# A one-core transformer block with 32 streamed experts: weights packed in load order, the router on the residual's own sums, one modulation sum on ScalarE and GpSimd

## The chip, the cores and the metric

The kernel runs on one core of a Trainium2 chip (trn2). The metric is the device time of one launch in microseconds (us). The kernel before takes 1129.11 us, the median of 3 runs (1129.04 to 1129.2). The engines are named as the profile names them: PE (TensorE), PEld (its weight loads), DVE (VectorE), ACT (ScalarE), POOL (GpSimd) and SP (SyncE, which here only issues DMAs).

## What is computed

One block over 256 tokens of width 1024: a modulated mixer (attention with forget gates, gated linear attention, a multi-scale pool), a layer norm, a top-4 mixture of 32 experts, a second layer norm. All in float32. Cut to what matters:

```python
mod = silu(c) @ w_ada + b_ada                # 6 vectors of 1024
shift1, scale1, gate1, shift2, scale2, gate2 = split(mod, 6)
h = x * (1 + scale1) + shift1
y = hybrid_mixer(h, w_in, ..., w_out)        # z = h @ w_in; attention, GLA, pool; @ w_out
x = layer_norm(ALPHA * x + (1 + gate1) * y, ln1_g, ln1_b)
h = x * (1 + scale2) + shift2
y = moe_ffn(h, w_router, w_gate_up, w_down)  # top 4 of 32 experts by h @ w_router + b_router
x = layer_norm(ALPHA * x + (1 + gate2) * y, ln2_g, ln2_b)
```

The experts' weights (32 times a gate/up matrix of 1024x2048 and a down matrix of 1024x1024) are 402 of the 449 MB that the kernel moves.

## The kernel before, in words

All tokens sit on the core as 2 tiles of 128 (`TT = 2`, `t`), the width as 8 slices of 128 (`KT = 8`, `k`). A matmul goes through the helper `mm` (L134 in the profile, L156 after the change).

The stages, with their tiles:
- **First layer.** `load_ada1` brings the columns of `w_ada` for shift1 and scale1, `load_z1` rows of `w_in`; `tokens_to_columns` transposes x on PE (`xT`), `modulate` makes hT = h transposed, and a loop over k adds up `pqk` (q and k of the attention) and `pz`. `second_part(0)` and `second_part(1)` do the remaining columns of `w_in` (`pz20n`, `pz21n`, weights `wz2_0`, `wz2_1`).
- **Mixer.** Scores `sc0` (first 128 queries) and `sc1`, their row maxima `mx0`, `mx1`, exponentials on ACT with row sums (L490), normalisation on DVE (L491, L492), transposes `ppT0` to `ppT5` on PE, outputs `po`; the gated linear attention with states `st`/`sts`, masks `at0`, `at1` (L599) and outputs `pg0`, `pg1`.
- **Modulation sums.** shift2 and scale2 (`accm0`, `accm1`, weights `adam0`, `adam1`), gate1 (`acc1`, weights `adag1`) and gate2 (`g2p`, weights `adag2`) are each a sum over 8 slices, `acc += w_k * cond_k`: one multiplication, then 7 `scalar_tensor_tensor` (STT) on DVE (L546, L624). `pcol0` and `pcol1` are 8 small matmuls each that turn accm0 and accm1 into columns; `m2`, `hA`, `hB` (L550 to L553) are made from them.
- **Out projection and router.** `py` is the product with `w_out` (`wo0`, `wo1`), then the residual and the first norm to `n1`, transposes `ph`, modulated columns `h2T`, logits `plg`, top 4, positions of the tokens in each expert's slots (`posm`), counts.
- **Experts.** 16 pairs of experts. `dispatch` builds a 0/1 matrix `pp` and gathers a pair's tokens by matmul (`pxg`, then `xg`), `gate_up` makes `gu`, `down` makes `py`, `combine` adds into `ya`.

Every engine runs its instructions in one fixed order, which a scheduler sets when the program is built, from the written program and its dependencies; it is not the order of the source. An instruction that waits holds up everything behind it on its engine. SP's order is that of the loads in the source. A load into a ring buffer waits until the last reader of that buffer's earlier content is done. The ring has `NA = 5` buffers of 2 MB; from the experts on a second pool, `ring2`, adds `NB = 3` in the memory that the earlier stages leave.

The expert loads go on SP: four `g` (gate/up, `load_up`, L737) and two `d` (down, `load_down`, L742) of 2 MB for each expert, which wait only for buffers.

Of the kernel before, what the change touches and what calls it, by code (L numbers as in the profile page):

```python
# [104 lines left out]

def packed_rows(b_ada, ln1_g, ln1_b, ln2_g, ln2_b):
# [6 lines left out]
def block_kernel(ctx: ExitStack, tc, x, w_ada, w_in, gla_w_a2, pool_w, w_out, w_router, w_gate_up, b_gate_up,  # L113
# [48 lines left out]

    half = const.tile([P, 8], F32, name="half")
# [13 lines left out]


    with tc.tile_pool(name="early", bufs=1) as ea, tc.tile_pool(name="late", bufs=1, side="right") as la_, \
# [9 lines left out]
        def load_ada1(cc):  # L189
            t = ring_tile(f"ada1_{cc}")  # L190
            if cc == 0:
                t = t.rearrange("p (a k s n) -> p a k s n", a=2, k=KT, s=2)
                ada.append(t.rearrange("p a k s n -> p a k (s n)"))
                return [lambda a=a: [SY.dma_start(t[:, a, :, h], w_ada[0, :, h * D + a * P:h * D + (a + 1) * P]
                                                  .rearrange("(k p) n -> p k n", p=P)) for h in range(2)]
                        for a in range(2)]
# [4 lines left out]
            ada.append(t.rearrange("p k s n -> p k (s n)"))  # L201

        def load_z1(k):
            if k % 2 == 0:
                wz1.append(ring_tile(f"wz1_{k // 2}")[:, 0:2 * (C_FV + Z1)].rearrange("p (k n) -> p k n", k=2))
            t = wz1[-1][:, k % 2]
            SY.dma_start(t[:, 0:W1], w_in[0, k * P:(k + 1) * P, 0:W1])
            SY.dma_start(t[:, W1:], w_in[0, k * P:(k + 1) * P, C_GA:])

        def load_cols(j, nm):  # L210
            ts = []
            for i in range(2):
# [25 lines left out]
        bgf = []  # L238
        for h in range(2):
            bgf.append(la_.tile([96, 2, 512], F32, tag=("acc", "g1p")[h], name=f"bgf{h}"))  # L240
            for j in range(3):
                SY.dma_start(bgf[h][32 * j:32 * j + 32], b_gate_up[0, 16 * h:16 * h + 16]
# [21 lines left out]
        ada_m.append(load_cols(4, "adam1"))  # L264
        wo = {}
        for i, ks in enumerate(((0, 1, 2, 6), (7, 3, 4, 5))):
            t = ring_tile(f"wo{i}").rearrange("p (k n) -> p k n", n=D)
            for j, k in enumerate(ks):
                wo[k] = t[:, j]
            j, k = (0, 0) if i == 0 else (1, 3)  # L270
            SY.dma_start(t[:, j:j + 3], w_out[0, k * P:(k + 3) * P, :].rearrange("(k p) n -> p k n", p=P))
            j, k = (3, 6) if i == 0 else (0, 7)
            SY.dma_start(t[:, j], w_out[0, k * P:(k + 1) * P, :])
        SY.dma_start(wr.rearrange("p (i k) n -> p i k n", k=2), w_router[0].rearrange("(i p k) n -> p i k n", p=P, k=2))
# [15 lines left out]
        for h in range(2):  # L290
            three_terms(bg3[:, 2 * h:2 * h + 2], bgf[h])
# [8 lines left out]
        hT = la_.tile([P, KT, S], F32, tag="hT", name="hT")  # L300
# [48 lines left out]
        for k in range(KT):  # L349
# [19 lines left out]
        z2 = la_.tile([P, TT, ZN - O_GV], F32, name="z2")  # L369
# [10 lines left out]
        z_gv = z2[:, :, 0:GVW]  # L380
        z_gr = z2[:, :, GVW:]
# [689 lines left out]
```

## Time and profile before

| | us |
|---|---|
| median of 3 runs | 1129.11 (1129.04 to 1129.2) |
| the profiled execution, its own time | 1129.8 |
| its span on the core | 1128.0 |
| PE busy in the span | 1035.4 (92%) |
| DVE / ACT / POOL busy | 318.7 (28%) / 98.8 (9%) / 41.5 (4%) |
| mean granted PE clock | 0.982 of full speed |
| HBM read | 447.67 MB, mean 398 GB/s over the span |

Times in the rows are us from the start of the span. In a timeline row the first number is the start, the second how long the stretch lasted, then the engine, the line, the operation, the output and inputs by name, shapes and how many; in brackets the idle time before it and what ended it. Busy shares are averages over stages with different limits; what holds the kernel up must be read stage by stage.

### The profile page before, as it was taken

What the parts mean: (1) busy time and instruction counts of PE and PEld (TensorE: products, weight loads), DVE (VectorE), ACT (ScalarE), POOL (GpSimd) and SP (SyncE); (2) the same over time, 40 slices, a digit from 0 to 9 for tenths busy, and PEclk for the clock granted to TensorE, in tenths of its full rate; (3) what the DMA queues carried; (4) which work ended last, traced back from release to release, by engine and by line L of the source; (5) the groups of instructions that cost most, each with busy time, mean ns of one, the idle gap of its engine ahead of it and who ended that gap; (6) DMA issues with size and microseconds to landing.
All of it is one profiled execution on the core that took longest, in us unless ns stands there. A gap on an engine that the chain in (4) does not pass through costs nothing.

```text
span 1128.0 us, 11046 instructions
## 1 busy us (share of the span) xinstructions
PE 1035.4 (92%) x4734; PEld 436.9 (39%) x4735; DVE 318.7 (28%) x587; ACT 98.8 (9%) x205; POOL 41.5 (4%) x43
## 2 busy tenths in 40 slices
PE   6999998999999999996999999989989898989795
PEld 3656545434333333333344343423333333333231
DVE  1459694322222122211122221213221121211113
ACT  1024112100000000000000000000000000000100
POOL 2270000000000000000000000000000000000000
PEclk9999897999999999998999999999999999999998
DMA  9997499999999999999899999999999999999992
GB/s 324 348 385 283 181 378 373 428 423 428 428 428 427 428 428 428 428 427 423 344 427 428 428 428 426 428 427 428 428 428 427 428 429 427 428 427 428 428 414 92
DMA packets 52998, 449.49 MB, mean 398 GB/s; under 512 B 5056, under 2 KB 18768, under 8 KB 28496
## 3 DMA queue, kind: packets, MB, share of 16 engines
q1 hardware_dynamic: 52320, 447.90, 95.7%
q8 instruction: 39, 0.64, 0.2%
q10 hardware_dynamic: 624, 0.83, 0.2%
q14 instruction: 15, 0.12, 0.0%
HBM read 447.67 MB, written 1.05 MB: 398 GB/s over the span
## 4 chain that ended last, share of the span: by engine, by line
PE 29%; DMA 22%; DVE 1%; issue 1%; ACT 0%; POOL 0%; DVEq 0%; POOLq 0%
DMA d<-in_w_down 22%; PE gu L134 13%; PE py L134 7%; PE pxg L134 4%; PE ya L134 3%; PE pyl L134 1%; PE paT L837 1%; DVE yb L855 0%; DVE aT L839 0%; DVE res L919 0%; ACT n L931 0%; PE pln L134 0%; DVE r L1038 0%; DVE yl L1015 0%; DVE st L1019 0%
## 5 line engine op out<-in xcount | busy, mean ns | idle before, releaser
L134 PE MATMUL gu<-g,xg 128*64 128x512 f32 x2048 | 462.5, 595 | 14.0 <-DMA g<-in_w_gate_up 12.6
L134 PEld LDWEIGHTS gu<-g,xg 128*64 128x64 f32 x2048 | 143.2, 137 | 295.5 <-issue 261.0
L134 PE MATMUL py<-d,aT 128*64 128x512 f32 x992 | 227.1, 600 | 13.8 <-DMA d<-in_w_down 12.5
L825 DVE TENSOR_SCALAR g<-gu 128x512 f32<-128x512 f32 x32 | 22.1, 692 | 410.1 <-PE gu L134 410.1
L134 PEld LDWEIGHTS py<-d,aT 128*64 128x64 f32 x992 | 70.0, 137 | 150.5 <-issue 140.8
L134 PE MATMUL pxg<-pp,n 128*128 128x128 f32 x512 | 77.0, 302 | 14.9 <-DVE aT L839 7.0
L134 PEld LDWEIGHTS pxg<-pp,n 128*128 128x128 f32 x512 | 69.2, 208 | 43.0 <-issue 29.6
L855 DVE TENSOR_TENSOR yb<-py,g2p 64x512 f32<-64x512 f32 x60 | 41.3, 689 | 139.0 <-PE py L134 138.4
L134 PE MATMUL ya<-yb,sg_None 128*128 128x512 f32 x120 | 58.2, 607 | 4.9 <-DVE yb L855 4.8
L829 ACT ACTIVATE s<-g 128x512 f32<-128x512 f32 x32 | 20.2, 630 | 464.4 <-DVE g L825 464.4
L793 DVE TENSOR_SCALAR xg<-pxg,hA,hB 128x128 f32<-128x128 f32 x64 | 25.8, 409 | 99.2 <-PE pxg L134 90.0
L791 ACT ACTIVATE xg<-pxg,hB,hA 128x128 f32<-128x128 f32 x64 | 28.7, 457 | 274.3 <-DVE xg L793 273.6
L134 PE MATMUL pz<-wz,hT 128*128 128x512 f32 (+2 forms) x128 | 52.4, 547 | 0.0
L169 POOL TENSOR_TENSOR rsb<-rtb,half 128x2 f32<-128x2 f32 x1 | 0.7, 701 | 950.9 <-DVE rtb L168 950.9
L839 DVE COPY aT<-paT 128x512 f32<-128x512 f32 x32 | 22.1, 692 | 43.9 <-PE paT L837 43.8
L134 PE MATMUL py<-wo,oT 128*128 128x512 f32 x64 | 30.9, 629 | 0.2 <-ACT oT L642 0.2
L134 PEld LDWEIGHTS ya<-yb,sg_None 128*128 128x128 f32 x120 | 20.4, 189 | 26.9 <-issue 17.4
L134 PEld LDWEIGHTS pz<-wz,hT 128*128 128x128 f32 x128 | 23.4, 190 | 17.3 <-issue 14.3
L837 PEld LDWEIGHTS paT<-kc,l 128*128 128x128 f32 x128 | 18.0, 209 | 25.3 <-DVE l L831 15.4
L837 PE MATMUL paT<-kc,l 128*128 128x128 f32 x128 | 23.7, 308 | 0.0
L831 DVE TENSOR_TENSOR l<-l,s 128x512 f32<-128x512 f32 x32 | 22.1, 691 | 3.4 <-DVE l L830 0.5
L134 PE MATMUL pqk<-hT,wz 128*128 128x256 f32 x96 | 22.2, 381 | 0.7 <-DVE hT L332 0.7
(245 smaller groups left out, 519.1 us busy)
## 6 DMA issues: line engine op xcount, KB each, us to landing
g<-in_w_gate_up SPq DMA_DIRECT2D x128, 2048.0 KB, 30.4
d<-in_w_down SPq DMA_DIRECT2D x62, 2048.0 KB, 30.4
adam<-in_w_ada SPq DMA_DIRECT2D x4, 2048.0 KB, 16.7
adag<-in_w_ada SPq DMA_DIRECT2D x4, 2048.0 KB, 9.0
ada<-in_w_ada SPq DMA_DIRECT2D x6, 1024.0 KB, 11.1
wz<-in_w_in SPq DMA_DIRECT2D x8, 760.0 KB, 9.5
wo<-in_w_out SPq DMA_DIRECT2D x2, 1536.0 KB, 10.0
ada<-in_w_ada SPq DMA_DIRECT2D x4, 512.0 KB, 7.4
```

Source lines behind the costliest of these rows:

```text
L134: T.matmul(o, l, r, start=start, stop=stop, skip_group_check=True, **kw)
L169: G.tensor_tensor(o, t[:, :n], half[:, :n], op=OP.pow)
L791: A.activation(xg[:, k], bs[k // 4][:, k % 4], AF.Identity, bias=hB[:, k:k + 1], scale=hA[:, k:k + 1])
L793: V.tensor_scalar(xg[:, k], bs[k // 4][:, k % 4], hA[:, k:k + 1], hB[:, k:k + 1], op0=OP.mult, op1=OP.add)
L825: V.tensor_scalar(g, gu[:, 0], LIMIT, None, op0=OP.min)
L829: A.activation(s, g, AF.Sigmoid, scale=SW_ALPHA)
L831: V.tensor_mul(l, l, s)
L837: T.transpose(b[:, j], act[:, j::4], ident)
L839: V.tensor_copy(aT, b)
L855: V.tensor_mul(yb[m * CAP:(m + 1) * CAP, n * 512:(n + 1) * 512], b[r], g2p[r, n * 512:(n + 1) * 512])
```

## The change

1. **Packed weights.** The host lays `w_ada`, `w_in` and `w_out` out by partition, in the order of the loads, so that each load is one DMA with one long run for each partition; x also comes transposed (`xT`), and the 16 transposes of `tokens_to_columns` go. x itself (`xs`) is loaded later, on SP between `adam1_1` and `wo0`.
2. **Modulation sums.** accm0 and accm1 are written earlier in the source. accm1 is no longer summed on DVE: ACT multiplies all 8 slices (`summed_by_two`), POOL adds 7 times. The first slice of acc1 and g2p is multiplied on ACT, not on DVE. m2, hA and hB are written later in the source, after the gated linear attention.
3. **Router on sums.** The transposes `ph` are taken from the residual before the norm, the norm's mean and scale are put in behind the logits: `wr2` is the router weight times hA and hB, `wrs` its sum, `prow` a row of constants. `h2T` is a plain copy, and the 16 modulations of it go.
4. **First pair.** The first pair's gather (`pxgA`, `ppA`, `xgA`) runs tile by tile inside the router's loop.
5. **Rings.** In each turn of 8 loads, numbers 3 to 5 now go to `ring2` (before: the last 3).

```diff
-            i = int(turn[0] % (NA + NB) >= NA)
+            i = int(3 <= turn[0] % (NA + NB) < 3 + NB)
...
-            t = t.rearrange("p (k s n) -> p k s n", k=KT, s=2)
-            for h in range(2):
-                SY.dma_start(t[:, :, h], w_ada[0, :, h * D + cc * 256:h * D + (cc + 1) * 256]
-                             .rearrange("(k p) n -> p k n", p=P))
+            SY.dma_start(t, w_ada[:, cc * 4096:(cc + 1) * 4096])
...
-            SY.dma_start(t[:, 0:W1], w_in[0, k * P:(k + 1) * P, 0:W1])
-            SY.dma_start(t[:, W1:], w_in[0, k * P:(k + 1) * P, C_GA:])
+            SY.dma_start(wz1[-1][:, k % 2], w_in[:, k * WZ:(k + 1) * WZ])
...
-        SY.dma_start(xs[:, :, 0:256], xv[:, :, 0:256])
+        SY.dma_start(hT[:, 0:2], xTv[:, 0:2])
         load_z1(0)
-        SY.dma_start(xs[:, :, 256:], xv[:, :, 256:])
         first_ada[1]()
+        SY.dma_start(hT[:, 2:], xTv[:, 2:])
...
         ada_m.append(load_cols(4, "adam1"))
+        SY.dma_start(xs, x[0].rearrange("(t p) d -> p t d", p=P))
...
+        def summed(acc, ts):
+            A.mul(acc, ts[0][:, 0], cond[:, 0:1])
+            for k in range(1, KT):
+                V.scalar_tensor_tensor(acc, ts[k // 4][:, k % 4], cond[:, k:k + 1], acc, op0=OP.mult, op1=OP.add)
+
+        def summed_by_two(acc, ts):
+            for k in range(KT):
+                w = ts[k // 4][:, k % 4]
+                A.mul(acc if k == 0 else w, w, cond[:, k:k + 1])
+                if k:
+                    G.tensor_add(acc, acc, w)
+
+        summed(accm[0], ada_m[0])
+        summed_by_two(accm[1], ada_m[1])
...
+        wr2 = la_.tile([P, 2, KT, NE], F32, tag="qin", name="wr2")
+        for j, h in enumerate((hA, hB)):
+            V.tensor_mul(wr2[:, j], wr, h[:, :, None].to_broadcast([P, KT, NE]))
+        wrs = la_.tile([P, 2, NE], F32, name="wrs")
+        V.tensor_reduce(wrs, wr2.rearrange("p j k e -> p j e k"), axis=AX.X, op=OP.add)
...
+                for j in range(4):
+                    T.transpose(b[:, j], twos(xs[:, t], 4 * n + j), ident)
+                A.copy(h2T[:, 4 * n:4 * n + 4, t * P:(t + 1) * P], b)
...
+            for k in range(KT):
+                mm(b[:, 0:NE], h2T[:, k, t * P:(t + 1) * P], wr2[:, 0, k], k == 0, k == KT - 1)
+            V.scalar_tensor_tensor(lg[:, t], b[:, 0:NE], rs, row, op0=OP.mult, op1=OP.add)
...
+            one_hot(ppA, posm[:, :, 0:2], t)
+            gathered(first, ppA, t)
+        modulated(xgA, first)
```

How the change moves instructions, at three places. First DVE, around the normalisation of `sc1`, which the transposes `ppT0` to `ppT5` wait for. Before:

```order
L410 TENSOR_TENSOR z2_398<-pz201_615,zb_137 128x384
L531 COPY qT_599<-pqT_600 64x2x256 [waits PE_49]
L546 SCALAR_TENSOR_TENSOR accm1_655<-adam1_0_154,cond_71,accm1_655 128x1024 [waits DMAHW0_49,Activation_49]
L491 RECIPROCAL sm1_559<-sm1_559 128x6 [waits DVE_49,Activation_49]
L546 SCALAR_TENSOR_TENSOR accm1_655<-adam1_0_154,cond_71,accm1_655 128x1024 [waits DVE_49]
L492 TENSOR_TENSOR sc1_509<-sc1_509,sm1_559 128x1536 [waits DVE_49]
L410 TENSOR_TENSOR z2_398<-pz211_625,zb_137 128x384 [waits PE_49]
L550 TENSOR_TENSOR m2_635<-pcol0_645,colv_61 128x8 [waits PE_49]
```

With the change:

```order
L530 TENSOR_TENSOR sc0_496<-sc0_496,sm0_518 128x768 [waits DVE_49]
L557 SCALAR_TENSOR_TENSOR qin_558<-z1_359,eb_556 128x4x48 [waits Activation_49]
L430 TENSOR_TENSOR z_gr_361<-pz211_613,zb_125 128x384 [waits PE_49]
L653 TENSOR_TENSOR m2_776<-pcol0_777,colv_61 128x8 [waits PE_49]
L653 TENSOR_TENSOR m2_776<-pcol1_787,colv_61 128x8 [waits PE_49]
L654 TENSOR_TENSOR hA_66<-m2_776,colv_61 128x8 [waits DVE_49]
L655 TENSOR_TENSOR hB_67<-m2_776,colv_61 128x8
L656 TENSOR_TENSOR hB_67<-hB_67,m2_776 128x8 [waits DVE_49]
L529 RECIPROCAL sm1_547<-sm1_547 128x6 [waits Activation_49]
L530 TENSOR_TENSOR sc1_497<-sc1_497,sm1_547 128x1536 [waits DVE_49]
L552 TENSOR_TENSOR kin_560<-z1_359,tmp_564 128x8x48 [waits Activation_49]
```

The reading of `pcol1` (the last term of m2) and hA, hB now stand ahead of the normalisation of `sc1`, though the source writes them after the gated linear attention; before, `pcol1` was read 12 rows behind it.

Then PE at the same place. Before, `pcol0` and the first transposes of the probabilities (`pcol1` came 29 rows further down):

```order
L134 MATMUL pz211_625<-wz2_1_152,hT_199 128x384 x6
L134 MATMUL pcol0_645<-kc_63,accm0_636 128x4 x8
L560 MATMUL ppT0_678<-kc_63,sc0_508 128x128 [waits Activation_49]
L562 MATMUL ppT0_678<-kc_63,sc1_509 128x128 [waits DVE_49,Activation_49]
L562 MATMUL ppT0_678<-kc_63,sc1_509 128x128
```

With the change:

```order
L156 MATMUL pz211_613<-wz2_1_141,hT_89 128x384
L156 MATMUL pcol0_777<-kc_63,accm0_425 128x4 x8
L156 MATMUL pcol1_787<-kc_63,accm1_426 128x4 [waits Pool_49]
L156 MATMUL pcol1_787<-kc_63,accm1_426 128x4 x7
L566 MATMUL pebT_581<-kc_63,eb_556 128x128 [waits Activation_49]
L566 MATMUL pebT_581<-kc_63,eb_556 128x128 x2
L566 MATMUL pkT_597<-kc_63,kin_560 128x128 [waits DVE_49,PE_49]
L566 MATMUL pkT_597<-kc_63,kin_560 128x128 x3
L586 MATMUL ppT0_633<-kc_63,sc0_496 128x128 [waits Activation_49]
```

`pcol1` now waits for POOL's last add, and the transposes of eb, k and the probabilities are queued behind it.

Last ACT, from the first exponential on. Before:

```order
L490 ACT_TABLE_LOAD
L490 ACTIVATE sc0_508,sm0_530<-sc0_508,mx0_528 128x128 [waits DVE_49]
L490 ACTIVATE sc0_508,sm0_530<-sc0_508,mx0_528 128x128 x5
L512 ACTIVATE eb_568<-pb_577 128x4x48 [waits PE_49]
L512 ACTIVATE eb_568<-pb_577 128x4x48
```

With the change:

```order
L528 ACT_TABLE_LOAD [waits DVE_49]
L528 ACTIVATE sc0_496,sm0_518<-sc0_496,mx0_516 128x128 [waits Pool_49]
L467 ACTIVATE accm1_426<-adam1_0_143,cond_71 128x1024 [waits DMAHW4_49]
L467 ACTIVATE adam1_0_143<-adam1_0_143,cond_71 128x1024 [waits DMAHW3_49,DMAHW0_49]
L467 ACTIVATE adam1_0_143<-adam1_0_143,cond_71 128x1024 x2
L528 ACTIVATE sc0_496,sm0_518<-sc0_496,mx0_516 128x128 x5
L550 ACTIVATE eb_556<-pb_565 128x4x48 [waits PE_49,Pool_49]
L467 ACTIVATE adam1_1_145<-adam1_1_145,cond_71 128x1024 [waits DMAHW7_49,DMAHW5_49,Activation_49]
```

The multiplications of accm1 come behind the first exponential, so behind `mx0`, and the table load waits for `mx0` as well.

## Rows read from the trace of the kernel before

**Rows 1.** Page, section 2: rates in 40 slices of 28.2 us.
```profile
GB/s 324 348 385 283 181 378 373 428 423 428 428 428 427 428 428 428 428 427 423 344 427 428 428 428 426 428 427 428 428 428 427 428 429 427 428 427 428 428 414 92
```

**Rows 2.** SP's issues of `g` and `d`, each with its time to landing.
```profile
L737 SPq DMA_DIRECT2D g<-in_w_gate_up x1: 430/430/430, 166.1 to 166.1; - x1
DMA to landing us min/median/max: 25.4/25.4/25.4
...
L742 SPq DMA_DIRECT2D d<-in_w_down x1: 328/328/328, 190.9 to 190.9; - x1
DMA to landing us min/median/max: 7.6/7.6/7.6
```

**Rows 3.** Timeline of DVE: normalisation of `sc1` and mask of `at1`.
```profile
107.20 1.75 DVE L492 TENSOR_TENSOR sc<-sc,sm 128x1536 f32<-128x1536 f32 x1
...
133.35 0.73 DVE L599 COPY_PREDICATED at<-kc,at 128x512 f32<-128x512 uint32 x1
```

**Rows 4.** Timeline of PE, first layer: transposes of x (first, last of four), last matmul.
```profile
8.10 1.12 PE L338 MATMUL xT<-kc,n 128*128 128x128 f32 x4
...
43.65 0.60 PE L338 MATMUL xT<-kc,n 128*128 128x128 f32 x4
...
67.36 3.60 PE L134 MATMUL pz<-wz,hT 128*128 128x512 f32 x8
```

**Rows 5.** Timeline of DVE: gate logarithms, accm0's first STT, mx0, normalisation of sc0.
```profile
74.26 1.85 DVE L426 TENSOR_SCALAR neg<-lin 128x396 f32<-128x396 f32 x1
...
80.91 1.28 DVE L546 SCALAR_TENSOR_TENSOR accm<-adam,cond,accm 128x1024 f32<-128x1024 f32 x1
...
94.89 0.95 DVE L487 TENSOR_REDUCE mx<-sc 128x6 f32<-128x768 f32 x1
...
99.14 0.95 DVE L492 TENSOR_TENSOR sc<-sc,sm 128x768 f32<-128x768 f32 x1
```

**Rows 6.** Timeline of POOL: bias preparation, and an add of the last norm.
```profile
55.11 1.03 POOL L282 CAST bg<-bgf 96x1024 bf16<-96x1024 f32 x1 [21.68 <-DMA bgf<-in_b_gate_up]
...
73.77 2.12 POOL L286 TENSOR_TENSOR bgf<-bgf,bg 32x1024 f32<-32x1024 f32 x1
...
1121.46 1.41 POOL L1038 TENSOR_TENSOR r<-r,n 128x512 f32<-128x512 f32 x1 [0.83 <-ACT r L1037]
```

**Rows 7.** Timeline of DVE beside that last add.
```profile
1122.03 1.40 DVE L1038 TENSOR_TENSOR r<-r,n 128x512 f32<-128x512 f32 x1 [0.28 <-ACT r L1037]
1123.35 0.74 DVE L1040 SCALAR_TENSOR_TENSOR r<-r,rsb,n 128x512 f32<-128x512 f32 x1
```

**Rows 8.** Timeline of ACT: table load, exponentials of sc0 and sc1, a modulation product, sg.
```profile
89.78 1.28 ACT L490 ACT_TABLE_LOAD   x1
95.87 0.40 ACT L490 ACTIVATE sc<-sc,mx 128x128 f32<-128x128 f32 x1 [4.81 <-DVE mx L487]
...
99.68 1.17 ACT L544 ACTIVATE accm<-adam,cond 128x1024 f32<-128x1024 f32 x1
101.84 0.51 ACT L490 ACTIVATE sc<-sc,mx 128x256 f32<-128x256 f32 x1 [0.99 <-ACT accm L544]
...
111.83 0.84 ACT L573 ACTIVATE sg<-z 128x768 f32<-128x768 f32 x1
```

**Rows 9.** Timeline of PE: transposes of k, of the probabilities, and pcol1.
```profile
102.37 0.63 PE L528 MATMUL pkT<-kc,kin 128*128 128x128 f32 x4
...
109.47 0.31 PE L560 MATMUL ppT<-kc,sc 128*128 128x128 f32 x1
...
119.09 2.48 PE L134 MATMUL pcol<-kc,accm 128*128 128x4 f32 x16
```

**Rows 10.** Stretches: start:end, length, busy PE, PEld, DVE, ACT, POOL, PE clock, DMA, GB/s.
```profile
110.00:120.50 10.50, 8.69 (x57) 6.15 (x57) 7.97 (x9) 4.70 (x8) 0.00 (x0) 1.00 1.02 398
120.50:127.30 6.80, 6.80 (x16) 2.92 (x15) 2.62 (x9) 0.00 (x0) 0.00 (x0) 0.50 0.73 292
```

**Rows 11.** Page, section 5: modulation on DVE of one slice of 128 columns.
```profile
L793 DVE TENSOR_SCALAR xg<-pxg,hA,hB 128x128 f32<-128x128 f32 x64 | 25.8, 409 | 99.2 <-PE pxg L134 90.0
```

More of the change, by code (lines that the diff above doesn't have):

```diff
@@ L176, in layer_norm_stats, with one_hot, gathered, modulated @@
         return mv[:, 0:1], rs
+    def one_hot(pp, pcol, t):
+        V.tensor_tensor(pp[:, t], pcol[:, t, :, None].to_broadcast([P, 2, CAP]),
+                        iota1[:, None, :].to_broadcast([P, 2, CAP]), op=OP.is_equal)
+    def gathered(bs, pp, t):
+        for k in range(KT):
+            mm(bs[k // 4][:, k % 4], twos(n1[:, t], k), pp[:, t].rearrange("p a s -> p (a s)"),
+               t == 0 and k % 4 == 0, t == TT - 1)
+    def modulated(xg, bs):
+        for k in range(KT):
+            if k % 2:
+                A.activation(xg[:, k], bs[k // 4][:, k % 4], AF.Identity, bias=hB[:, k:k + 1], scale=hA[:, k:k + 1])
+            else:
+                V.tensor_scalar(xg[:, k], bs[k // 4][:, k % 4], hA[:, k:k + 1], hB[:, k:k + 1], op0=OP.mult, op1=OP.add)
     with tc.tile_pool(name="early", bufs=1) as ea, tc.tile_pool(name="late", bufs=1, side="right") as la_, \
@@ L264, in block_kernel @@
         ada_m.append(load_cols(4, "adam1"))
+        SY.dma_start(xs, x[0].rearrange("(t p) d -> p t d", p=P))
         wo = {}
[L266 to L274, printed above, removed]
+        for i in range(2):
+            t = ring_tile(f"wo{i}")
+            SY.dma_start(t, w_out[:, i * 4096:(i + 1) * 4096])
+            for j in range(4):
+                wo[WO_ORDER[4 * i + j]] = t[:, j * D:(j + 1) * D]
         ada_g1 = load_cols(2, "adag1")
@@ L538, in block_kernel @@
         second_part(1)
[L541 to L553 removed]
+        acc1 = la_.tile([P, D], F32, tag="acc", name="acc1")
+        summed(acc1, ada_g1)
         for m in range(3):
@@ L653, in block_kernel @@
         oh = []
+        ppA = la_.tile([P, TT, 2, CAP], F32, tag="kin", name="ppA")
         for t in range(TT):
@@ L702, in block_kernel @@
             V.scalar_tensor_tensor(posm[:, t], b[:, 0:NE], 1.0, msel[:, t], op0=OP.add, op1=OP.mult)
+            one_hot(ppA, posm[:, :, 0:2], t)
+            if t == 0:
+                first = [bank(f"pxgA{q}", "z").rearrange("p (j s) -> p j s", j=4) for q in range(2)]
+            gathered(first, ppA, t)
+        modulated(xgA, first)
         def finish_routing():
@@ L774, in weights @@
         return loaded.pop((kind, e))
+    evens = [str(i) for i in range(0, NE // 2, 2)]
     def dispatch(pcol, gcol, nm):
@@ L780, in dispatch @@
         for t in range(TT):
-            V.tensor_tensor(pp[:, t], pcol[:, t, :, None].to_broadcast([P, 2, CAP]),
-                            iota1[:, None, :].to_broadcast([P, 2, CAP]), op=OP.is_equal)
-        xg = wk.tile([P, KT, P], F32, tag="xg", name=f"xg{nm}")
-        bs = [mps.tile([P, 4, P], F32, tag="m", name=f"pxg{nm}_{q}") for q in range(2)]
-        for t in range(TT):
-            for k in range(KT):
-                mm(bs[k // 4][:, k % 4], twos(n1[:, t], k), pp[:, t].rearrange("p a s -> p (a s)"),
-                   t == 0 and k % 4 == 0, t == TT - 1)
-        for k in range(KT):
-            if k % 2:
-                A.activation(xg[:, k], bs[k // 4][:, k % 4], AF.Identity, bias=hB[:, k:k + 1], scale=hA[:, k:k + 1])
-            else:
-                V.tensor_scalar(xg[:, k], bs[k // 4][:, k % 4], hA[:, k:k + 1], hB[:, k:k + 1], op0=OP.mult, op1=OP.add)
+            one_hot(pp, pcol, t)
+        if nm == "0":
+            xg = xgA
+        else:
+            xg = xgA if nm in evens else wk.tile([P, KT, P], F32, tag="xg", name=f"xg{nm}", bufs=1)
+            bs = [mps.tile([P, 4, P], F32, tag="m", name=f"pxg{nm}_{q}") for q in range(2)]
+            for t in range(TT):
+                gathered(bs, pp, t)
+            modulated(xg, bs)
         def gates(m=None):
@@ L1027, in block_kernel @@
     stats = [(mv[:, t, 0:1], rs[:, t:t + 1]) for t in range(TT)]
-    r = [wk.tile([P, D], F32, tag="xg", name=f"r{t}") for t in range(TT)]
+    r = [xgA.rearrange("p k s -> p (k s)"), wk.tile([P, D], F32, tag="xg", name="r1", bufs=1)]
     for t in range(TT):
```

159 lines of the change are left out of this document (72 added, 87 removed).

## The prediction

> **What bounds the kernel now.** I read the page's rates by slice first [rows 1]. From the eighth of 40 slices on the core moves 423 to 428 GB/s in nearly every one. There the expert loads follow each other without a gap: 2 MB at 428 GB/s is 4.9 us a load, and PE, though busy, waits for them. No edit touches that part, so the end moves by what the start of this stream moves, and by what the stream loses once. The holes are in slices 4 and 5, 283 and 181 GB/s: there the mixer runs and SP has no buffer to load into. A loss that can go is the first `d` load [rows 2]: the `g` load issued at 166.1 lands 25.4 later, at 191.5; the `d` load is issued at 190.9, when PE has read the first `g` buffer, and lands at 198.5. That is 7.0 us after its forerunner, not 4.9: 2.1 us lost.
>
> So I follow the chain that frees the buffers. The second mask `at1` on DVE ends at 134.1 [rows 3]; what follows (gate1's sum, `py`, the loads of `g`) keeps its length behind it, within half a microsecond by the order of both kernels, since the same instructions follow in the same order. I use the end of `at1` as a mark and ask when it comes.
>
> The sum is made on the profiled execution, 1129.8 us with a span of 1128.0; the median is 1129.11, 0.7 lower, and I apply the shift to the median. About 0.2% (2.3 us) is what a measurement can tell from no change.
>
> **The first layer.** The change takes out 16 transposes of x on PE, in four groups of 1.12 down to 0.60 [rows 4], 3.0 us together by the four. PE is almost gapless there, so the loop ends that much earlier than 70.96. The packed first loads have no price in this trace; between nothing and 2 us, I take 1, as each only replaces two transfers of the same bytes. Gain 4.0, bounds 3 and 5.
> POOL's bias preparation starts at 55.1 on a DMA and still adds at 73.77; `neg` on DVE, issued at 74.26, ends at 76.11, just behind POOL's add at 75.89 [rows 5, 6]. With fewer DMAs ahead, those loads land earlier and the stall of 1.6 us goes. accm0's first STT comes at 75.3 instead of 80.9. Of the 5.6 us I carry 3.5 to `mx0` (bounds 2 and 5.6), because PE's score products stand between: `mx0` ends at 92.3, not 95.8.
>
> **The sum of accm1 on ACT and POOL.** DVE loses 7 STT of 1.28 [rows 5]. ACT now holds: table load 1.28, which was hidden ahead of `mx0` and now waits for it; one exponential 0.40, with some 0.2 for its sum (an estimate); two products of 1.17 [rows 8]. The first add can start at 92.3 + 4.2 = 96.5. POOL's add of 128x1024 isn't in this trace. Lower bound: 2.12, the add of 32x1024. Upper bound: 2.82, twice the 1.41 of 128x512 [rows 6]. I take 2.35, nearer to the row of the same length. Seven make 16.4.
> DVE and POOL can get in each other's way: POOL's add of 1121.46 ended at 1122.87, and a DVE operation with two SBUF inputs issued at 1122.03 took 1.40, where its like took 0.74 [rows 6, 7]. In the stretch of the adds DVE has the normalisation of sc0, 0.95 [rows 5], and two small ones; I add 0.8 (bounds 0 and 1.7). The last add ends at 113.7.
>
> **What waits for it.** In the new order PE's `pcol1` stands ahead of the transposes of k and of the probabilities, and on DVE the reading of `pcol1` ahead of the normalisation of sc1. Nothing of this needs accm1, but it is queued behind it. From the last add: pcol1 1.0 (its 2.48 holds half-clock work and waits [rows 9]), the small DVE operations 0.8 (an estimate), normalisation 1.75 [rows 3], k 0.5, its transposes 0.63 [rows 9]: 4.7. `ppT0` starts at 118.4 instead of 109.47, 8.9 later, and DVE's freed 9 us don't shorten this.
> From `ppT0` to the mark took 24.6 [rows 3, 9]. Of this 2.5 go, as pcol1 is done; 2.1 go, as the table load and `sg` (1.28 and 0.84 [rows 8]) now stand ahead of the first copy of probabilities; 0.4 come in with q's transposes: 20.4 if the clock behaves as before. That held one stretch of 6.8 us at a granted 0.50, 1.2 GHz, with PE busy throughout [rows 10], after a stretch in which PE was busy 8.7 of 10.5 us. Without it the mark comes 3.4 earlier.
> At 109.47 all that now stands ahead of pcol1 was done before, so PE will stand still for 4 us or more until 113.7, and I expect the low stretch again. The Trainium skill ("TensorE: Matmul & The Clock Gate", Part 1) says that the clock follows how busy PE has lately been; by that, too, the idle time would bring half clock into the transposes. The trace agrees as far as its low stretch follows gaps.
> Mark: 118.4 + 20.4 = 138.8, 4.7 later than 134.1.
>
> **Router, first pair, rings.** Out go the 16 modulations of `h2T`, half of them on DVE at 0.41 [rows 11], the logits' second transpose, and, with the gather tile by tile, half the first pair's gather from the path to the first gate/up product. Added (`wr2`, `wrs`, `prow`, `row`) lies beside the states and masks, off the path. This part shortens the way from the last `py` to the first `gu`, which matters to the stream only by the 2.1 us; more than 2.1 us seem safe, so they go (bounds 0 and 2.1). The ring numbers only change which loads wait; nothing else is gained once the stream runs. x loaded later, 1 MB ahead of `wo0`, falls in a full stretch and delays `wo` by 2.5 us; `wo` isn't wanted before the outputs, so 0.
>
> **Sum.** 4.7 later at the mark, the same at the start of the stream, 2.1 given back at `d`: +2.6, 1131.7 us. Its own range is 1130 to 1134: half a microsecond between mark and stream, 1.1 below and 2.1 above for the adds and the early part, within the bounds named.
>
> **Rivals.**
> - *Full clock behind the idle time.* The same, without 3.4: 1128.3, no change. For it: through 110 to 120.5, with 1.8 us of gaps in it, the clock stayed full [rows 10]; against it: the gap will be longer.
> - *POOL keeps pace with ACT* (faster). If an add costs about 1.03, as the cast of 96x1024 [rows 6], the last comes right behind ACT's last product: 96.5 + two products, five exponentials, eb, four products = 106. Then six exponentials of 0.5 [rows 8] bind, to 109.3; ppT0 at 112.3, 6.1 earlier than above: 1125.6, and 1122.2 at full clock. The two-operand adds of 2.12 speak against it; that POOL's time per column may hang on the operation (1.03 against 2.12 for 1024) speaks for it.
> - *The adds take longer, or the early part gains nothing* (slower). Seven at 2.82 add 3.3; the packed loads not landing earlier and `mx0` staying at 95.8 add 3.5. Either gives about 1135.1. It decides once the last add ends after 116.
> - *The router isn't 2.1 shorter.* Then the loss at `d` stays: +2.1 on any of these.
>
> By the Trainium skill ("SBUF — State Buffer", Who interferes with whom) a DVE instruction with two SBUF inputs and a GpSimd one that reads SBUF exclude each other for a whole instruction. The trace agrees (1.40 against 0.74, above). Counted in full for every such DVE operation, it would give 1132.6; I count half, for some will meet POOL between two adds.
>
> **How the numbers follow.** The forecast 0.36, full clock 0.20, POOL in pace 0.24, the slow one 0.20 (the router's loss is inside these). Slower by over 0.2% (above 1131.4): 0.22 of the forecast and the slow case, 0.42. Same: 0.14 of the forecast and 0.14 of full clock, 0.28. Faster: POOL in pace and the 0.06 left of full clock, 0.30. The range from 1123 to 1136 leaves out some 0.10 below and 0.07 above.
>
> **What would show it.** First layer's last `pz` at about 67; `mx0` at about 92; POOL's seven adds of 2.1 to 2.8 us, the last at 111 to 116; `pcol1` waiting for POOL and `ppT0` behind 116; a PE clock of 0.5 somewhere between 113 and 130; `at1` at 135 to 140; the first `d` load landing 4.9 behind the last `g`. I am wrong if `ppT0` starts before 113, if an add takes under 2 us, or if the stretch after 200 changes its pitch.

## The result, and the profile after

The changed kernel takes 1135.88 us (median of 4 runs, 1135.47 to 1138.96), the kernel before 1129.15 beside it: a ratio of 1.0063, 95% interval 1.0043 to 1.0082. It is slower by 0.63%, some 7 us. The forecast was slower by 2.6 us: the sign held and the range (1123 to 1136) just held the time, the size did not. The profiled execution took 1136.0 us with a span of 1134.2; before, 1129.8 and 1128.0.

The rates by slice, page section 2 of the changed kernel, answer to [rows 1]:

```profile
GB/s 368 380 327 322 153 228 420 426 426 430 426 429 427 425 430 427 426 428 426 359 428 427 428 428 427 428 426 429 428 425 430 427 425 430 426 426 428 428 415 96
```

The first two slices move more (368 and 380 for 324 and 348); slices 5 and 6 move less (153 and 228 for 181 and 378). The stream of expert loads starts later and then runs at the same pace. SP's issue of the last of the first eight `g` loads and the first `d` load, each with its time to landing (answers to [rows 2]):

```profile
L779 SPq DMA_DIRECT2D g<-in_w_gate_up x1: 327/327/327, 178.3 to 178.3; - x1
DMA to landing us min/median/max: 23.7/23.7/23.7
...
L784 SPq DMA_DIRECT2D d<-in_w_down x1: 328/328/328, 196.1 to 196.1; - x1
DMA to landing us min/median/max: 10.8/10.8/10.8
```

They land at 202.0 and 206.9, 4.9 apart: the gap of 7.0 us before is gone, as forecast. But the eighth load comes 10.5 us later than before, and the first `d` 8.4.

Now the chain that leads there. The timeline of PE in the first layer (start, length, engine, line, operation; [rows 4] before):

```profile
11.50 5.49 PE L156 MATMUL pqk<-hT,wz 128*128 128x256 f32 x12 [0.71 <-DVE hT L368]
...
22.22 1.90 PE L156 MATMUL pp<-ada,cond 128*32 128x512 f32 x4
...
26.84 1.93 PE L156 MATMUL pp<-ada,cond 128*32 128x512 f32 x12
...
67.63 3.60 PE L156 MATMUL pz<-wz,hT 128*128 128x512 f32 x8
```

And two rows of the kernel before, for the same products:

```profile
12.91 2.86 PE L134 MATMUL pqk<-hT,wz 128*128 128x256 f32 x12 [0.70 <-DVE hT L332]
...
22.35 1.95 PE L134 MATMUL pp<-ada,cond 128*32 128x512 f32 x16 [0.68 <-ACT hT L340]
```

The 16 transposes are gone, and the first products start 1.4 us earlier, but the loop ends at 71.2; before it was 70.96. Two things ate the gain. The same 12 matmuls that took 2.86 us before take 5.49, and they start 0.43 us apart, later ones 0.22: half clock. The trace's own record of the clock begins with a rise to full, at 17.3 us here and at 11.3 in the trace of before. And the 16 products `pp` of the second load of `w_ada`, which took 1.95 us in one go, now stand in two parts in PE's order, 4 ahead of the next `pqk` and 12 behind it, and take 1.90 and 1.93. In the trace of before four of them run beside each other (they start 0.01 to 0.02 us apart); the 4 that stand alone follow one another, 0.43 us apart. That is 1.9 us more of PE. No run takes this second cost away.

The timeline of DVE ([rows 3, 5] before):

```profile
74.53 0.37 DVE L446 TENSOR_SCALAR neg<-lin 128x396 f32<-128x396 f32 x1
...
78.99 1.28 DVE L461 SCALAR_TENSOR_TENSOR accm<-adam,cond,accm 128x1024 f32<-128x1024 f32 x1
...
95.22 0.94 DVE L525 TENSOR_REDUCE mx<-sc 128x6 f32<-128x768 f32 x1
...
104.25 1.71 DVE L525 TENSOR_REDUCE mx<-sc 128x6 f32<-128x1536 f32 x1
105.88 2.41 DVE L530 TENSOR_TENSOR sc<-sc,sm 128x768 f32<-128x768 f32 x1
108.21 2.49 DVE L557 SCALAR_TENSOR_TENSOR qin<-z,eb 128x192 f32<-128x192 f32 x1
...
122.22 1.76 DVE L530 TENSOR_TENSOR sc<-sc,sm 128x1536 f32<-128x1536 f32 x1
...
143.80 0.73 DVE L626 COPY_PREDICATED at<-kc,at 128x512 f32<-128x512 uint32 x1 [4.61 <-PE at L156]
```

The stall of `neg` is gone (0.37 for 1.85), `mx0` is no earlier (96.2 for 95.8). Then two DVE operations are stretched, both with two inputs in SBUF: the normalisation of sc0 (2.41 for 0.95) and `qin` (2.49; the same operation took 0.36 in the kernel before, at 98.86). The row maximum `mx1` just ahead of them has one input and is not stretched (1.71; 1.75 before). The normalisation of sc1 comes at 122.2 and not at 107.2, the mark (end of `at1`) at 144.5 and not at 134.1: 10.4 us later. What stands beside `mx1` and the two stretched operations is POOL's sum:

```profile
100.24 17.53 POOL L469 TENSOR_TENSOR accm<-accm,adam 128x1024 f32<-128x1024 f32 x7 [27.67 <-ACT adam L467]
```

The timeline of PE there, and one row of the kernel before (107.68), for the same 16 small matmuls at full clock:

```profile
110.85 0.45 PE L566 MATMUL pqT<-kc,qin 128*128 128x128 f32 x1 [3.57 <-DVE qin L557]
...
117.82 3.58 PE L156 MATMUL pcol<-kc,accm 128*128 128x4 f32 x16 [2.04 <-POOL accm L469]
...
124.59 1.09 PE L566 MATMUL pkT<-kc,kin 128*128 128x128 f32 x4 [2.45 <-DVE kin L552]
125.47 0.42 PE L586 MATMUL ppT<-kc,sc 128*128 128x128 f32 x1
```

```profile
107.68 1.94 PE L134 MATMUL pcol<-kc,accm 128*128 128x4 f32 x16
```

`ppT0` starts at 125.5; before, 109.5. And the stretches of the changed kernel (start:end, length, busy PE, PEld, DVE, ACT, POOL, PE clock, DMA, GB/s; [rows 10] before):

```profile
95.00:109.00 14.00, 11.31 (x42) 7.20 (x41) 8.54 (x12) 12.75 (x25) 8.52 (x4) 1.00 0.59 233
109.00:129.00 20.00, 13.66 (x55) 11.57 (x56) 8.84 (x18) 6.58 (x17) 9.52 (x6) 0.51 0.74 304
129.00:145.00 16.00, 15.99 (x90) 10.34 (x88) 7.44 (x15) 3.83 (x7) 0.00 (x0) 0.97 0.01 1
```

From 109 to 129 the granted clock is 0.51, 1.2 GHz. It fell while PE stood still for 3.57 us behind `qin`, from 107.3 to 110.9. Before, the low stretch lasted 6.8 us.

### The profile page after: what moved, and what is told of

Same layout as the page of the kernel before. It is cut to its first block, busy times and chain, and to the rows that moved or that the text cites. A ratio compares the mean times of both kernels' runs of the same rounds, so it can differ in the third digit from the quotient of the medians.

```text
span 1134.2 us, 11016 instructions
## 1 busy us (share of the span) xinstructions
PE 1034.3 (91%) x4718; PEld 439.9 (39%) x4719; DVE 307.4 (27%) x574; ACT 105.6 (9%) x208; POOL 57.4 (5%) x50
## 4 chain that ended last, share of the span: by engine, by line
DMA 25%; PE 25%; DVE 2%; issue 1%; ACT 0%; SPq 0%; POOL 0%; DVEq 0%; POOLq 0%; ACTq 0%
DMA d<-in_w_down 19%; PE gu L156 11%; PE py L156 6%; DMA g<-in_w_gate_up 6%; PE ya L156 3%; PE pxg L156 3%; PE pyl L156 1%; PE paT L877 1%; DVE yb L895 0%; DVE aT L879 0%; DVE res L959 0%; ACT n L971 0%; PE pln L156 0%; PE pl L156 0%; DVE yl L1055 0%
## 5 line engine op out<-in xcount | busy, mean ns | idle before, releaser
L156 PE MATMUL gu<-g,xgA 128*64 128x512 f32 x1024 | 231.9, 595 | 9.4 <-DMA g<-in_w_gate_up 7.0
L156 PE MATMUL gu<-g,xg 128*64 128x512 f32 x1024 | 230.6, 595 | 9.0 <-DMA g<-in_w_gate_up 9.0
L156 PEld LDWEIGHTS gu<-g,xgA 128*64 128x64 f32 x1024 | 72.0, 136 | 149.9 <-issue 129.8
L156 PEld LDWEIGHTS gu<-g,xg 128*64 128x64 f32 x1024 | 71.4, 137 | 149.9 <-issue 134.2
L156 PE MATMUL pxg<-pp,n 128*128 128x128 f32 x480 | 69.6, 293 | 12.6 <-DVE aT L879 7.1
L156 PEld LDWEIGHTS pxg<-pp,n 128*128 128x128 f32 x480 | 62.3, 200 | 40.2 <-issue 27.1
L156 PEld LDWEIGHTS ya<-yb,sg_None 128*128 128x128 f32 x120 | 20.4, 189 | 27.0 <-issue 17.4
L216 ACT ACTIVATE xgA<-pxg,hB,hA 128x128 f32<-128x128 f32 x28 | 12.6, 457 | 142.8 <-DVE xgA L218 142.5
L216 ACT ACTIVATE xg<-pxg,hB,hA 128x128 f32<-128x128 f32 x32 | 14.4, 457 | 121.8 <-DVE xg L218 121.5
L156 PE MATMUL pqk<-hT,wz 128*128 128x256 f32 x96 | 24.9, 414 | 0.7 <-DVE hT L368 0.7
```

The costliest lines, as they stand in the source:

```text
L156: T.matmul(o, l, r, start=start, stop=stop, skip_group_check=True, **kw)
L216: A.activation(xg[:, k], bs[k // 4][:, k % 4], AF.Identity, bias=hB[:, k:k + 1], scale=hA[:, k:k + 1])
```

## The experiments

Several chips ran them; the kernel before ran beside each, and ratios are against it on the same chip. Its runs there lie between 1125.7 and 1135.3 us, so a median over runs says less than the ratio with its interval and the times in the trace. A difference between ratios from two chips carries the intervals of both.

**1. pcol1 behind the attention outputs.**

```diff
-                mm(b[:, q], twos(acc, q), ones[:, 0:4], True, True)
+                w1 = ones[:, 0:4]          # j == 1: made as 0 * oT[:, 2, 0:4] + 1
+                mm(b[:, q], twos(acc, q), w1, True, True)
```

> The changed kernel with one edit: pcol1 multiplies by ones that are made from the attention output (0 times it plus 1), so it can't stand ahead of the transposes; ACT and POOL still make accm1. Theory (the place of pcol1 in PE's and DVE's order is the cost): ppT0 no longer waits for POOL's last add (117.8 in the changed kernel) but for the exponentials of sc1 (end at 111.5 there) and its normalisation, so it starts at 113 to 116 instead of 125.5, the at1 mask ends 8 to 11 us earlier than 144.5, and the time is 1125 to 1128. Rival (the sum on two engines costs by itself, through ACT's eight products ahead of the exponentials and through the DVE operations stretched beside POOL): ppT0 moves less than 4 us and the time stays above 1132.

Measured: 1.0035 (1.0015 to 1.0055), 1134.2 us. That is 0.28% below the change (the intervals overlap), and not the 0.7% to 1% that I gave to the place of pcol1. The theory fell, and both marks of the rival came: with nothing waiting for the last add, the trace still has `ppT0` at 122.8, and the time stays above 1132. The execution in the trace is one of the longest of this run, 1138.25 us, and `mx0` is 1.3 us later in it than in the change; but from the end of `mx0` to the end of `at1` it takes 48.3 us, and the change 48.4. So the trace shows no gain at the mark. The timeline of DVE shows what remains:

```profile
107.16 2.41 DVE L530 TENSOR_TENSOR sc<-sc,sm 128x768 f32<-128x768 f32 x1
109.49 2.50 DVE L557 SCALAR_TENSOR_TENSOR qin<-z,eb 128x192 f32<-128x192 f32 x1
...
117.35 3.31 DVE L530 TENSOR_TENSOR sc<-sc,sm 128x1536 f32<-128x1536 f32 x1
```

Three operations with two SBUF inputs wait beside POOL's adds (1.46, 2.14 and 1.55 us longer than alone); the third ends 1.6 us behind the last add (119.05), its own 1.76 of work. The place of pcol1 is at most a part; the adds themselves cost.

**2. accm1 summed on DVE.**

```diff
-        summed_by_two(accm[1], ada_m[1])
+        summed(accm[1], ada_m[1])
```

> The changed kernel with accm1 summed as accm0 is (one product on ACT, 7 multiply-adds of 1.28 us on DVE), at the changed place in the source. Theory: no wait for POOL and no DVE operation stretched beside it; 9 us of DVE work come back in the stretch of 100 to 115, so ppT0 at 110 to 113, at1 10 to 13 us earlier than 144.5, time 1123 to 1126. If it comes out within 1 us of the run with pcol1 late, the two-engine sum as such is worth nothing either way. Rival (the early part is the cost: mx0 no earlier, first layer no shorter): 1133 or more, since this edit doesn't touch it.

Measured: 0.9982 (0.9959 to 1.0006), 1128.5 us against 1129.8: 0.8% below the change, and with the rest of the change in place no slower than before, perhaps 0.2% faster. `ppT0` comes at 111.5, as expected; at1 at 135.2, not 131.5 to 134.5, and the time lies above the 1123 to 1126 as well. The timeline of DVE has the STT ahead of the normalisation, unstretched:

```profile
110.72 1.28 DVE L461 SCALAR_TENSOR_TENSOR accm<-adam,cond,accm 128x1024 f32<-128x1024 f32 x1
111.92 1.75 DVE L530 TENSOR_TENSOR sc<-sc,sm 128x1536 f32<-128x1536 f32 x1
```

**3. The ring rule of before.**

```diff
-            i = int(3 <= turn[0] % (NA + NB) < 3 + NB)
+            i = int(turn[0] % (NA + NB) >= NA)
```

> The changed kernel with the ring rule of before. It asks for the 2 us that the changed kernel regains on the way (196 loads: the first d load lands 8.4 us later than before, the last 6.4 later). Theory (those 2 us come from elsewhere): within 1 us of 1135.9. Rival (the new rule lets loads 3 to 5 go out early and saves the small gaps): 1137.5 to 1139.

Measured: 1.0061 (1.0033 to 1.0089), the same as the change; the median, 1137.8, is no use beside a kernel before at 1129.8. From the first `d` landing to the last, in the stretches of this run, of the change and of before:

```profile
209.30:1116.70 907.40, 844.96 (x3917) 326.22 (x3915) 192.95 (x348) 55.69 (x113) 0.00 (x0) 0.99 1.00 423
```

```profile
207.00:1113.00 906.00, 841.66 (x3912) 324.96 (x3912) 193.73 (x349) 55.81 (x113) 0.00 (x0) 1.00 1.00 423
```

```profile
198.50:1106.70 908.20, 846.51 (x3928) 326.92 (x3926) 193.87 (x349) 55.84 (x113) 0.00 (x0) 0.99 1.00 423
```

By landings it is 907.6, 906.3 and 908.3 us. The other traces add to this: the seven further runs with the new rule, and the change again (run 10), take 906.1 to 907.1, and run 4, with the rule of before, 907.8. The two groups don't overlap, so of the 2.0 us that the change regains on the way some 1.3 (run 3 against the change) go with the ring rule; the rest stays open. The time doesn't show it.

**4. The kernel before with the two-engine sum alone.**

```diff
-            for k in range(1, KT):
-                V.scalar_tensor_tensor(acc, ada_m[j][k // 4][:, k % 4], cond[:, k:k + 1], acc, ...)
+            for k in range(KT):            # j == 1
+                A.mul(w if k else acc, w, cond[:, k:k + 1])
+                if k:
+                    G.tensor_add(acc, acc, w)
```

> The kernel before with one part of the change alone: accm1 as eight products on ACT and seven adds on POOL. By its order pcol1 then stands between the first and second transposes of the probabilities on PE. Theory: the adds of 2.35 end at 113 to 118, ppT1 waits for them and pcol1, 6 to 10 us later than its 111.4, and the time is 1133 to 1138: this part alone makes the loss. Rival (the loss needs the other parts, the half clock in the first layer among them): under 1131.

Measured: 1.0069 (1.0044 to 1.0094), 1139.0 us. This part alone makes a loss as large as the whole change does. The marks came later than the theory had them: the last add ends at 123.8, and `ppT1` starts at 128.0. In the timeline of PE, pcol1 waits behind `ppT0` here, and the other transposes wait behind pcol1 (first two rows: the first 12 products of the first layer and its last):

```profile
14.13 5.49 PE L134 MATMUL pqk<-hT,wz 128*128 128x256 f32 x12 [0.70 <-DVE hT L332]
...
70.90 3.60 PE L134 MATMUL pz<-wz,hT 128*128 128x512 f32 x8
...
114.19 0.31 PE L565 MATMUL ppT<-kc,sc 128*128 128x128 f32 x1
...
123.89 3.58 PE L134 MATMUL pcol<-kc,accm 128*128 128x4 f32 x16 [6.47 <-POOL accm L551]
...
128.02 0.48 PE L565 MATMUL ppT<-kc,sc 128*128 128x128 f32 x1
```

So in this order it is mostly the wait for the last add (6.47 us of PE) that costs, and only one two-input operation on DVE is stretched by much. The first two rows show something else. The first layer here is that of the kernel before, with the transposes of x in it, and its first 12 products run at half clock all the same (5.49 us, the clock rising at 20.4); the loop ends at 74.5, and 3.0 us of the delay of the mark against the trace of before lie ahead of the edit.

**5 and 6. Without the adds, and with adds that nobody reads.** Both keep the changed kernel's order up to the transposes.

```diff
                 if k:
-                    G.tensor_add(acc, acc, w)
+                    G.tensor_add(w, w, w)      # run 6; run 5 leaves the add out
```

> The changed kernel without POOL's seven adds; accm1 is then only ACT's first product (the sum over the other slices is left out), and the order on every other engine stays as in the changed kernel. What is left of the two-engine sum is ACT's eight products ahead of the exponentials of sc1. Theory now (POOL's adds cost twice, by the wait of pcol1 for the last one and by DVE operations with two SBUF inputs that stand still beside them; ACT's products cost little): normalisation of sc0 back at 0.95 us, no PE gap from 108 to 111, no half clock ahead of ppT0, ppT0 at 113 to 115.5, at1 10 to 12 us earlier than in the changed kernel, time 0.7% to 1.0% below it, that is 3 to 5 us below the kernel before. Rival (ACT's products, 8.5 us ahead of the exponentials, are the cost): ppT0 stays at 118 or later.

> The changed kernel with the seven adds in place, of the same size and at the same time, but each into its own product (w + w), so that nothing waits for the last one; pcol1 reads ACT's first product (the sum over the other slices is left out). Order as in the changed kernel. It holds the standstill of DVE beside POOL without the wait of pcol1. Theory (both count, some 3 us for the standstill with the half clock behind it, the rest for the wait): ppT0 at 117 to 121, time between the run without adds and the changed kernel, 2 to 5 us above the former. Rival 1 (the wait is all): within 1 us of the run without adds. Rival 2 (the standstill is all): within 1.5 us of the changed kernel's 0.6% above before.

Measured: without adds 0.9977 (0.9955 to 0.9999), unread adds 1.0034 (1.0009 to 1.0059). The adds cost 0.57% even when nobody waits for them, and here the intervals, from one chip, don't overlap. The change lies 0.29% higher still, with run 10 0.25%; those intervals overlap. The first rival of run 6 falls; the second isn't excluded by the time alone. The theory had put too little on the standstill: the time is 6.4 us above run 5 (2 to 5 expected), and `ppT0` starts at 123.6 (117 to 121). The timelines of DVE, without adds and with them unread, and POOL's of the latter:

```profile
106.63 0.95 DVE L528 TENSOR_TENSOR sc<-sc,sm 128x768 f32<-128x768 f32 x1
107.50 0.35 DVE L555 SCALAR_TENSOR_TENSOR qin<-z,eb 128x192 f32<-128x192 f32 x1
...
114.54 1.76 DVE L528 TENSOR_TENSOR sc<-sc,sm 128x1536 f32<-128x1536 f32 x1
```

```profile
106.45 2.62 DVE L530 TENSOR_TENSOR sc<-sc,sm 128x768 f32<-128x768 f32 x1
108.99 2.04 DVE L557 SCALAR_TENSOR_TENSOR qin<-z,eb 128x192 f32<-128x192 f32 x1
...
120.35 1.76 DVE L530 TENSOR_TENSOR sc<-sc,sm 128x1536 f32<-128x1536 f32 x1
```

```profile
100.81 13.82 POOL L469 TENSOR_TENSOR adam<-adam 128x1024 f32<-128x1024 f32 x7 [28.06 <-ACT adam L467]
```

Two operations, 1.30 us together, take 4.66: 3.4 us of standstill, and `qin` ends 3.2 us later. PE waits for it (3.32 us), falls to half clock, and the 32 matmuls of both pcols, which took 4.95 us without adds, take 6.83. So the normalisation of sc1 is 5.8 us later and at1 6.1 (142.6 for 136.5). The unread add reads one tile twice and takes 1.89 (the median), not 2.35, so this is, if anything, a little under what the real adds do.
Of run 5's marks two came: the normalisation of sc0 takes 0.95, and PE has no gap from 108 to 111. `ppT0` starts at 117.8, not at 113 to 115.5 and close to the rival's 118, and at1 is 8.0 us earlier than in the change, not 10 to 12. The time is 0.86% below the change, as expected, but 2.6 us below before and not 3 to 5. The pcols, at half clock from 111.1, end at 113.7, and the normalisation of sc1 stands behind their reading. The exponentials of sc1 end at 112.2 (104.9 before), so ACT's products would be the next to bind; what they cost by themselves no run shows.

One measure leaves out what happens ahead of `mx0`: the time from its end to the end of `at1`. It is 38.2 us before, 38.8 in run 2, 39.6 without adds, 45.9 with unread adds, 46.7 in run 4, 47.4 in run 10 and 48.4 in the change. Of the 10 us by which the change lengthens this way, 6.3 come with adds that nobody reads, and 1.5 to 2.5 more with the wait for them and their greater length.

**7. accm1 on DVE behind the normalisation of sc1, both pcols behind the attention outputs.**

```diff
+        V.scalar_tensor_tensor(cond2, ss[1][:, 0, 0:KT], 0.0, cond, op0=OP.mult, op1=OP.add)
+        summed(accm[1], ada_m[1], cond2)
...
+            V.tensor_scalar(w1, oT[:, 2, 0:4], 0.0, 1.0, op0=OP.mult, op1=OP.add)
+                mm(b[:, q], twos(acc, q), w1, True, True)
```

> The changed kernel with accm1 back on DVE, and its multiply-adds tied behind the normalisation of sc1 (their factor is cond plus 0 times a normalised score), pcol0 and pcol1 tied behind the attention outputs (ones made from them). With accm1 on DVE alone, 7 STT of 1.28 us stood ahead of the normalisation, which ended at 113.7. Theory (whatever stands ahead of that normalisation on DVE sets ppT0): it ends at 107 to 110, ppT0 at 108 to 110, at1 3 to 6 us earlier than the 135.2 of that run, and the time is 2 to 5 us below it, 0.3% to 0.6% below before. Rival (PE, ACT's copies or the load of gate1's weights bind behind it): within 1 us of that run.

Measured: 1.0065 (1.0042 to 1.0089), 1136.4 us: a miss, for the rival too. The normalisation did come early, it ends at 107.8, and ppT0 at 108.8, as the theory said; at1 comes at 133.3, only 1.9 us earlier than in run 2. But the freed chain ran into two others. This is read from the trace; no run takes the two edits apart. Timelines of PE and ACT, and a stretch:

```profile
121.96 0.85 PE L156 MATMUL kv<-z_gv,kout 64*128 64x192 f32 x4 [2.94 <-DVE sts L616]
...
132.22 6.83 PE L156 MATMUL pcol<-w,accm 128*128 128x4 f32 x32
```

```profile
135.67 1.15 ACT L459 ACTIVATE acc<-adag,cond 128x1024 f32<-128x1024 f32 x1 [4.72 <-PE pcol L156]
```

```profile
135.00:145.00 10.00, 10.00 (x43) 7.61 (x45) 3.65 (x6) 1.15 (x1) 0.00 (x0) 0.50 0.00 0
```

The STT now stand ahead of the states `sts` on DVE; PE waits 2.94 us for them and is at half clock from 122.9 to 150.2, in the stretch shown with nothing idle. And gate1's sum writes into accm0's buffer, so it waits for pcol0, which I had moved back: it ends at 155.5, as late as in the change (155.8). The early ppT0 was worth nothing here.

**8. PE kept busy ahead of the first layer.**

```diff
+        V.memset(warm, 1.0)
+        for i in range(4):
+            mm(bw, warm[:, 0:P], warm, True, True)
         modulate(0, 1)
```

> The changed kernel with four products of 128x512 ones ahead of the first pp on PE (added work, unused). In the changed kernel the first 12 matmuls of pqk start 0.43 us apart, and later ones 0.22: half clock at the start, 2.7 us of PE time, where before they ran at full clock behind the transposes of x. Theory: with PE busy ahead of it the first pqk run at 0.22, the first layer's loop ends 2 to 3 us earlier than 71.2, the adds start 2 to 3 earlier than 100.2, and the time falls by 2 to 3 us. Rival (loads of weights, not PE, then bind the loop): loop end within 0.7 us of 71.2, time unchanged.

Measured: 1.0033 (1.0008 to 1.0058), 0.30% below the change, some 3.4 us, though the intervals overlap. The first products run at full clock (the clock rises at 5.7 us), the loop ends at 68.8, `mx0` at 93.7, at1 3.4 us earlier than in the change. The timeline of PE:

```profile
1.53 5.76 PE L156 MATMUL warm<-warm 128*128 128x512 f32 x8 [1.53 <-DVE warm L371]
...
10.21 2.83 PE L156 MATMUL pqk<-hT,wz 128*128 128x256 f32 x12 [0.77 <-DVE hT L368]
...
19.45 1.88 PE L156 MATMUL pp<-ada,cond 128*32 128x512 f32 x4 [1.32 <-DMA ada<-in_w_ada]
...
65.19 3.60 PE L156 MATMUL pz<-wz,hT 128*128 128x512 f32 x8
```

The rival is partly right: PE waits 1.3 us for a load up to 19.45 and 0.3 for one at 21.65, so not all of what was freed comes through.

**9 and 10. Both good edits together, and the change again beside it.** Run 9 is run 2 and run 8 in one.

> The changed kernel with accm1 on DVE and the four products of ones ahead of the first pp: the two edits that helped apart from each other (0.18% below before, and 2.4 us off mx0). Theory (they add up, since one lies in the first layer and the other behind mx0): mx0 at 93.5 to 94.2, at1 2 to 3.5 us earlier than 135.2, time 0.3% to 0.5% below before. Rival (behind an earlier mx0 the load of adam1 or PE's half clock binds, or the stream can't start earlier): within 0.1% of the run with accm1 on DVE alone.

> The changed kernel as it is, beside the others on the same chip. Theory: 0.5% to 0.75% above before, POOL's first add at 100 to 102 and its last at 117 to 119, sc0's normalisation over 2 us, at1 at 143 to 147. If it comes out under 0.4%, half of what the single parts were given is spread between chips and not their own.

Measured: run 9 0.9966 (0.9951 to 0.9982), 1124.7 us: faster than both kernels, if only by 0.34% than the one before. `mx0` ends at 93.6, at1 at 133.4, 1.8 us earlier than in run 2 (2 to 3.5 were expected):

```profile
92.66 0.94 DVE L530 TENSOR_REDUCE mx<-sc 128x6 f32<-128x768 f32 x1
...
132.63 0.73 DVE L631 COPY_PREDICATED at<-kc,at 128x512 f32<-128x512 uint32 x1 [4.61 <-PE at L156]
```

The change again 1.0059 (1.0038 to 1.0079), 1135.6, with at1 at 144.5. On one chip, then, the two edits together are worth 0.93%. What the products of ones add to run 2 is 0.16% by the ratios, whose intervals overlap.

## Why the prediction was half right

By its own steps, against the profile after:

- **What bounds it; the mark.** Right as the thing to follow. The stream kept its pace, the mark came 10.4 later, the first loads of `g` 8.4 to 10.5 later.
- **The loss at the first `d`.** Right in the number: 2.1 us given back, the landings 4.9 apart. From the mark to the issue of the first `d` it is 51.5 us, before 56.8, so the way is shorter by more than the 2.1. That this was needed is not shown: in run 4, with the router of before, it is 55.1 and the landings are 5.2 apart all the same (there the eighth `g` came 11.6 later than before, and the issue of `d` only 9.7).
- **The first layer, "gain 4.0", and "`mx0` ends at 92.3".** Wrong, and the step that failed, with the largest error: the loop's end came 0.3 later instead of 4.0 earlier, and `mx0` at 96.2, 3.9 later than forecast. The step took 3.0 us of transposes off PE and priced the work left at the durations of the one trace of before. Two terms were missing. First, the clock: in that trace it rose at 11.3 us, and the first 12 products took 2.86; in the changed kernel it rose at 15.2 to 17.5 in all eight of its traces without added products, and in the change they took 5.49. Run 8 shows what this is worth: with PE busy ahead of them, the loop ends 2.4 us earlier. It would be wrong to say that the transposes had kept the clock full, for run 4 has them, and its first products take 5.49 as well. Beside that trace (loop end at 74.5) the changed first layer, at 71.2, is 3.3 us shorter, near the forecast. So the base was at fault as much as the gain; why the clock rose so early in the one trace of before is open. Second, the order: the `pp` products in two parts cost 1.9 us. The stall of `neg` went as forecast, 1.5 us, but accm0's first STT came at 79.0 and not at 75.3, and nothing of it reached `mx0`, which PE's chain behind the loop decides.
- **The adds.** Right in size: 2.35 us was the median of the seven (one took 2.94, beside a DVE operation), 17.5 from first to last; the sum had 17.2. The first started 4.1 behind `mx0`; the sum had 4.2.
- **From the last add to ppT0, "4.7".** 7.7 us. pcol1 took 3.58 and not 1.0. At full clock the same 16 take 1.94, which is in the trace of before, at pcol0; I had read it off a row with waits in it and guessed low. The rest is half clock.
- **ppT0 to the mark, "20.4".** 19.1, with a low stretch, as forecast, but earlier and longer than I had it: 20 us, from 109, most of it ahead of `ppT0`.
- **Sum.** 3.9 - 0.1 + 0.3 + 3.0 - 1.3 is 5.8, but for rounding the 5.7 by which the mark (144.5) lies behind the forecast 138.8. The stream gave back 2.0 on its way that the forecast didn't have (some 1.3 of it by the ring rule, see run 3), and the span grew by 6.2. That the range still held the time is in part luck: these 2.0 and the 1.3 came off what the first layer and the wait had put on.
- **What it forecast for the cause.** pcol1 in front of the transposes was, in the changed kernel's order, the smaller part: 0.25% to 0.29% by the change against run 6, not clear of noise, and nothing at the mark in run 1's trace. (In run 4's order the wait is the larger one.) The standstill of DVE beside POOL, for which I added 0.8 us to POOL's side, is the larger, 0.57% by runs 5 and 6: it isn't POOL that is late by it, but `qin`, and PE behind `qin`. The Trainium skill ("SBUF — State Buffer", Who interferes with whom) states this exclusion for whole instructions, and the trace agrees: 0.95 became 2.41 to 2.62, and 0.35 became 2.04 to 2.50. I had counted it on the wrong engine.
- **The rivals.** "POOL keeps pace with ACT" fell with the first add. "Full clock behind the idle time" fell: 0.51 from 109 to 129. "The adds take longer, or the early part gains nothing" gave 1135.1 by its second half; its sign came, the last add after 116 (117.8), and that half is what happened, though not by the loads, as I had it, but by the clock and the order of `pp`; that its number lies so near the measured 1135.9 is luck too, for the reasons under the sum. "The router isn't 2.1 shorter" fell.

## What to carry to other kernels

A sum moved from DVE to POOL isn't free for DVE: as long as POOL adds from SBUF, each DVE operation with two SBUF inputs may wait for most of an add (up to 2.14 of 2.35 us here), so look which of these lie in that stretch and who waits for them. Before pricing PE's first products from one trace, look when the clock rose in it, and whether another execution of the same code has it there too; a few products that nobody reads, put ahead of them, brought the first layer's end forward by 2.4 us here. Look up in the built order, too, whether products that ran beside each other still stand together. And a sum that is wanted late should be looked up in each engine's built order, not in the source: what stands behind it there waits with it, and its buffer may be wanted earlier than its value.

## What the runs showed of the hardware

- In the mixer, in seven traces (the change, runs 1, 3, 6, 7, 8, 10), the clock fell in or just behind a wait of PE of 2.9 to 3.6 us, and the low stretch lasted 17 to 27 us although PE was often busy (10.0 of 10 us at 0.50 in run 7). In run 4 it fell behind two waits of 1.5 and 1.6 us, for 17.1. It fell without any wait over 1.5 us in the 20 us ahead as well: before and in run 2 for 6.8 us, in runs 5 and 9 for 10.2.
- In the first layer the profile's clock column says 1.00 while the matmuls start at half pace (0.43 us for 256 columns). The trace's record of the clock begins with the first rise (11.3 us before, 20.4 in run 4, 15.2 to 17.5 with the changed first layer, 5.7 and 5.6 with the products of ones), and the column shows 1.00 for the time ahead of it; there the pitch of the matmuls tells the clock, the column doesn't.
- A POOL add of 128x1024 with two different inputs takes 2.35 us, with the same tile twice 1.89 (medians); the rows of the trace of before had given 2.12 to 2.82 as its bounds.
